# Products of a tile of zeros ahead of the first dense column and in the last norm

## The chip, the cores and the metric

The kernel runs on one core of a Trainium2 chip. The metric is the time of one execution on the device in microseconds (us); several executions are timed, and one is recorded by the profiler. The engines of the core are TensorE (PE, the matrix engine, whose weight loads are shown as PEld), VectorE (DVE), ScalarE (ACT), GpSimd (POOL) and SyncE (SP), which here issues nearly all DMAs. Each engine works through its own instructions in order.

## What is computed

Two layers of a decoder trunk on 512 tokens of width 1024, with 256 memory tokens; batch 1, all in f32. Cut to what matters:

```
for l in range(2):
    h = rmsnorm(x, norm_mix[l])
    p = h @ w_in[l]                        # columns: MLA | HGRN2 | S5 | RWKV-7 | 4 merge gates
    o_mla, o_hg, o_s5, o_rw = ...          # four token mixers on p, each 512 wide
    gates = sigmoid(gate_logits)           # 4 x 1024 columns of p
    y = (gates[0] * (o_mla @ w_branch_mla[l]) + gates[1] * (o_hg @ w_branch_hgrn[l])
         + gates[2] * (o_s5 @ w_branch_s5[l]) + gates[3] * (o_rw @ w_branch_rwkv[l]))
    x = x + y @ w_out[l]
    x = x + cross_attn(rmsnorm(x, norm_xq[l]), rmsnorm(mem, norm_xm[l]), ...)
    x = x + conv_ffn(rmsnorm(x, norm_ffn[l]), ...)
return rmsnorm(x, norm_final)
```

`mla` is causal latent attention with 4 heads: per head the scores of 4 query blocks of 128, a softmax, the transposed probabilities times the values.

## The kernel before

Activations lie transposed: a tile is 128 features by 512 tokens, 8 tiles for the width of 1024. All dense layers go through `dense`: the weights arrive in chunks of 8 blocks of 128 x 128 (`raw`, 512 KB, 3 buffers) in the one order in which they are used, ACT copies a chunk to a rounded half `whi` (L236), DVE makes the rest `wlo` (L237), and PE forms three products a block, L329 (`whi` times the high half of the activations), L330 (`whi` times the low half) and L331 (`wlo` times the high half). A column of 8 blocks is 24 products into one of two PSUM banks `mm`.

`run` begins with the load of the first chunk, the memory tokens (`mt`, halves `mh` and `ml`), and the 8 key columns of the memory for layer 0 (`early_keys`), whose products are 256 wide. `mixers` then walks the columns of the input projection in a fixed order; the mixers hang on it with priorities. After the mixers' columns come those of the gates (`gate`: copied by ACT at L556 to `g`, stored to `g_d`). `mla` runs when its columns are there. Its last steps for a head are: the softmax into the tiles `pr0` to `pr3`, transposes (L1574) into PSUM, copies `mpT` by ACT (L1575), four products with the values (L1578, bank `rwy`), a copy `mo` by ACT (L1580) and its store to `o_d[0]` in device memory.

`merge` follows. For each of the four mixers, in the order HGRN2, RWKV-7, MLA, S5, it loads the four tiles of the output (`oin`, 2 buffers), splits them into `oh` (ACT, L359) and `ol` (DVE, L360), loads a gate tile `gin` per column, applies a sigmoid on ACT (L574), and forms 8 columns of 4 blocks each. After it come cross attention, the feed-forward part, and in the end `final`: squares of `x`, four products with `ones` (L385), a short chain on DVE, four products that broadcast the result (L401), a scaling of 8 tiles and their stores.

A scheduler sets the order of all engines: it takes instructions by priority (by default their place in the code) as soon as it reckons them ready, so that work without inputs can stand far from where the code has it. Tiles live in pools. The constants, the activation halves, the ring of weights and the pools of the stages are stacked from the left of SBUF; some pools, that of `merge` (`mg`) among them, are stacked from the right. A pool whose memory was used by an earlier pool waits until that one is released, that is, until the last instructions that use its tiles are done. The pool of `mla` (`ml`) is on the left.

Of the kernel before, what the change touches and what calls it, by code (L numbers as in the profile page):

```python
# [9 lines left out]
F32 = mybir.dt.float32  # L10
# [12 lines left out]
P = 128  # L23
# [187 lines left out]
class Ring:  # L211


    def __init__(self, T, name, pool, raw_bufs, bufs):
        self.T, self.name, self.pool, self.rb, self.b = T, name, pool, raw_bufs, bufs
        self.n = CHUNK[name]
        self.order, self.dram, self.pos = ORDERS[name], T.A[name], 0
        self.raws = {}
# [32 lines left out]
class Trunk:  # L251
    def __init__(self, ctx, tc, A):
        self.tc, self.nc, self.A, self.ctx = tc, tc.nc, A, ctx
        nc = self.nc
        self.const = self.pool(ctx, "const")
        self.const.tile([P, 48], F32, name="pad0")
        self.hp = self.pool(ctx, "hp")
        self.sm = self.pool(ctx, "sm")
        self.sm.tile([P, 56], F32, name="pad1")
        self.pool(ctx, "pr", side="right").tile([P, 24], F32, name="pad2")  # L260
        self.ps = self.pool(ctx, "ps", space=PSUM)
        self.ring = Ring(self, "w", self.pool(ctx, "ring"), 3, 2)
        self.vec = self.const.tile([P, L, NVEC], F32, name="vec")
        nc.sync.dma_start(out=self.vec, in_=A["vec"])
        self.halves = self.const.tile([P, L, 24], F32, name="halves")
        o = VOFF["w0"]
        nc.vector.tensor_scalar(out=self.halves, in0=self.vec[:, :, o:o + 24], scalar1=0.5, scalar2=None, op0=ALU.mult)
        self.ident = self.const.tile([P, P], F32, name="ident")
        self.ones = self.const.tile([P, 1], F32, name="ones")
        nc.vector.memset(self.ones, 1.0)  # L270
        dp = self.pool(ctx, "dram", space=bass.MemoryType.DRAM)
        self.r_d = [dp.tile([3, 4, P, S], F32, name=f"r_d{l}") for l in range(L)]
        self.xk_d = [dp.tile([KD, P, MEM], F32, name=f"xk_d{l}") for l in range(L)]
        self.c_d = dp.tile([3, P, S], F32, name="c_d")
        self.su_d = dp.tile([4, P, 4, P], F32, name="su_d")
        self.sy_d = dp.tile([4, P, 4, P], F32, name="sy_d")
        self.x_d = dp.tile([KD, P, S], F32, name="x_d")
        self.o_d = [dp.tile([4, P, S], F32, name=f"o_d{m}") for m in range(4)]
        self.g_d = dp.tile([4, 8, P, S], F32, name="g_d")
# [420 lines left out]
    def ffn(self, l, pool):  # L700
# [3 lines left out]
        for half in range(2):  # L704
# [21 lines left out]
            for n in range(8):  # L726
                ps = self.dense([("down", l, half * FHALF + k, n) for k in range(FHALF)], lambda k: act[k])
                self.residual(ps, n)

    def final(self, out):  # L730
        nc = self.nc
        rs = self.rstd(self.x, D, S, self.xp)
        for j in range(KD):
            t = self.x[j]
            nc.vector.scalar_tensor_tensor(out=t, in0=t, scalar=self.v(0, "norm_final", j), in1=rs,
                                           op0=ALU.mult, op1=ALU.mult)
            self.dma(out[j], t)

    def run(self, out):
        A = self.A  # L740
        with ExitStack() as c:
            self.ring.load(0)
            kv = self.pool(c, "kv0")
            self.dma(self.ident, A["ident"])
            self.memory(0, kv, bufs=8)
            self.ring.load(1)
            self.xp = self.pool(c, "xp0")
            self.load_x(A["xT"], 2)
            self.early_keys(0, kv)
            with self.first(E0):  # L750
                self.norm_scaled(0, "norm_mix")
            self.constants(self.xp)
        for l in range(L):
            self.mixers(l)
            with ExitStack() as c:
                with ExitStack() as c2:
                    with ExitStack() as c3:
                        self.merge(l, self.pool(c3, "mg", side="right"))
                    self.xp = self.pool(c, "xp")
                    self.load_x(self.x_d if l else A["xT"])  # L760
                    kv = self.pool(c2, "kv")
                    self.memory(l, kv, True)
                    self.xk = [kv.tile([P, KD, MEM], F32R, name=f"xk{i}") for i in range(2)]
                    self.xv = [kv.tile([P, 2, D], F32R, name=f"xv{i}") for i in range(2)]
                    for n in range(8):
                        self.key_tile(l, kv, n)
                    for half in range(XV0[l]):
                        self.values(l, half)
                    for n in range(8):
                        ps = self.dense([("out", l, k, n) for k in range(KD)], self.h)  # L770
                        self.residual(ps, n)
                    with ExitStack() as c3:
                        self.xattn(l, kv, self.pool(c3, "xa", side="right"))
                with ExitStack() as c2:
                    self.ffn(l, self.pool(c2, "ff", side="right"))
                if l + 1 < L:
                    with ExitStack() as c2:
                        kv = self.pool(c2, "kv0")
                        self.memory(l + 1, kv)
                        self.early_keys(l + 1, kv)  # L780
                    for j in range(KD):
                        self.dma(self.x_d[j], self.x[j])
                    self.norm_scaled(l + 1, "norm_mix")
                else:
                    self.final(out)
# [891 lines left out]
```

## Time and profile before

| | us |
|---|---|
| median of 3 runs | 2731.95 (2727.4 to 2735.38) |
| the profiled execution | 2726.05 |
| its span, first to last instruction | 2724.2 |
| PE busy | 2662.7, 98% of the span |
| PE weight loads busy | 2168.2, 80% |
| DVE busy | 1816.5, 67% |
| ACT busy | 1114.3, 41% |

A row of the instructions in order of time reads: start in us, duration in us, engine, line, operation, output <- inputs, shape, count; in brackets the idle time of the engine ahead of it and what ended it. Matmuls overlap, so the distance between two starts tells the pace and not the duration.

### The profile page before, as it was taken

How to read it: one execution, taken by the hardware profiler on the slowest of the kernel's cores; microseconds unless marked ns; L12 is line 12 of the kernel's file. 1: busy time of each engine (PE TensorE's matmuls, PEld its weight loads, DVE VectorE, ACT ScalarE, POOL GpSimd, SP SyncE). 2: the span in 40 equal slices, each digit the busy share in tenths (PEclk: the TensorE clock that was granted, in tenths of full speed). 3: DMA queues.
4: the chain of work that ended last, by engine and by line, in shares of the span. 5: the costliest groups of instructions: out<-in, count | busy, mean ns of one | idle time of the engine just before them, and what ended most of it. 6: DMA issues, size and time to landing. Idle time of an engine off the chain costs nothing.

```text
span 2724.2 us, 37420 instructions
## 1 busy us (share of the span) xinstructions
PE 2662.7 (98%) x13920; PEld 2168.2 (80%) x13920; DVE 1816.5 (67%) x3826; ACT 1114.3 (41%) x1796; POOL 32.6 (1%) x117
## 2 busy tenths in 40 slices
PE   7999999999999999999999999999999999999997
PEld 6778877787788888888887787777877788888886
DVE  6588878876585566446475887888665945664563
ACT  5333353336654443223243334344465634332231
POOL 1000000000000000000000000000000000000000
PEclk9999999999999999999999999999999999999999
DMA  6332143344673233332443232333555632332332
GB/s 207 96 93 77 43 130 92 110 144 156 224 223 115 85 93 100 94 101 93 128 145 104 85 90 71 117 96 122 158 177 179 212 98 70 93 101 93 101 94 77
DMA packets 140134, 319.11 MB, mean 117 GB/s; under 512 B 20656, under 2 KB 42800, under 8 KB 139952
## 3 DMA queue, kind: packets, MB, share of 16 engines
q1 hardware_dynamic: 139952, 316.72, 37.3%
q8 instruction: 110, 1.80, 0.3%
q14 instruction: 72, 0.59, 0.1%
HBM read 266.06 MB, written 45.61 MB: 114 GB/s over the span
## 4 chain that ended last, share of the span: by engine, by line
PE 81%; DVE 10%; DMA 4%; ACT 2%; issue 2%; SPq 1%; DVEq 0%; POOL 0%; ACTq 0%; POOLq 0%
PE mm L330 20%; PE mm L329 20%; PE mm L331 20%; DVE wlo L237 2%; PE rw L1033 2%; PE hg L1396 1%; SPq L319 1%; DVE rdg L941 1%; PE rwy L658 1%; PE rw L658 1%; PE rw L1561 1%; DVE rdg L943 1%; ACT whi L236 1%; PE rw L1052 1%; PE mm L352 1%
## 5 line engine op out<-in xcount | busy, mean ns | idle before, releaser
L329 PE MATMUL mm<-hh,whi 128*128 128x512 f32 x2144 | 850.4, 397 | 3.4 <-ACT wa L471 2.5
L330 PE MATMUL mm<-hl,whi 128*128 128x512 f32 x2144 | 850.4, 397 | 0.0
L331 PE MATMUL mm<-hh,wlo 128*128 128x512 f32 x2144 | 849.0, 396 | 0.0
L236 ACT ACTIVATE whi<-raw 128x1024 fp32r<-128x1024 f32 (+1 forms) x402 | 417.8, 1040 | 740.0 <-PE mm L330 636.4
L237 DVE TENSOR_TENSOR wlo<-raw,whi 128x1024 fp32r<-128x1024 f32 (+1 forms) x402 | 481.3, 1198 | 294.0 <-ACT whi L236 287.8
L329 PEld LDWEIGHTS mm<-hh,whi 128*128 128x128 f32 x2144 | 404.3, 189 | 86.5 <-ACT wa L471 2.9
L330 PEld LDWEIGHTS mm<-hl,whi 128*128 128x128 f32 x2144 | 404.3, 189 | 83.1 <-issue 1.6
L331 PEld LDWEIGHTS mm<-hh,wlo 128*128 128x128 f32 x2144 | 404.4, 189 | 80.3 <-issue 1.5
L329 PE MATMUL mm<-ah,whi 128*128 128x512 f32 x352 | 136.9, 389 | 0.0
L330 PE MATMUL mm<-al,whi 128*128 128x512 f32 x352 | 136.9, 389 | 0.0
L331 PE MATMUL mm<-ah,wlo 128*128 128x512 f32 x352 | 136.9, 389 | 0.0
L587 DVE TENSOR_TENSOR x<-mm,x 128x512 f32<-128x512 f32 x64 | 44.2, 690 | 122.3 <-PE mm L331 122.3
L329 PE MATMUL mm<-oh,whi 128*128 128x512 f32 x256 | 100.9, 394 | 0.9 <-ACT mh L362 0.4
L331 PE MATMUL mm<-oh,wlo 128*128 128x512 f32 x256 | 100.1, 391 | 0.0
L330 PE MATMUL mm<-ol,whi 128*128 128x512 f32 x256 | 100.0, 391 | 0.0
L710 DVE TENSOR_TENSOR gt<-mm,rstd 128x512 f32<-128x512 f32 x44 | 30.5, 692 | 98.6 <-PE mm L331 94.7
L941 DVE TENSOR_TENSOR rdg<-rdg,rE 128x2 f32<-128x2 f32 (+30 forms) x248 | 83.9, 338 | 3.4
L717 ACT ACTIVATE cv<-cv 128x512 f32<-128x512 f32 x44 | 27.8, 632 | 129.7 <-DVE cv L715 129.7
L331 PEld LDWEIGHTS mm<-ah,wlo 128*128 128x128 f32 x352 | 66.1, 188 | 13.7
L329 PEld LDWEIGHTS mm<-ah,whi 128*128 128x128 f32 x352 | 66.1, 188 | 13.7
L330 PEld LDWEIGHTS mm<-al,whi 128*128 128x128 f32 x352 | 66.1, 188 | 13.7
L720 DVE TENSOR_TENSOR up<-mm,rstd 128x512 f32<-128x512 f32 x44 | 30.4, 691 | 63.9 <-PE mm L331 63.9
(516 smaller groups left out, 4008.9 us busy)
## 6 DMA issues: line engine op xcount, KB each, us to landing
raw<-w SPq DMA_DIRECT2D x384, 512.0 KB, 3.5
g_d<-g SPq DMA_DIRECT2D x64, 256.0 KB, 2.1
gin<-g_d SPq DMA_DIRECT2D x64, 256.0 KB, 3.7
oin<-o_d SPq DMA_DIRECT2D x32, 256.0 KB, 3.7
mt<-memT SPq DMA_DIRECT2D x32, 128.0 KB, 3.5
x<-xT SPq DMA_DIRECT2D x16, 256.0 KB, 5.4
raw<-wm SPq DMA_DIRECT2D x10, 256.0 KB, 2.8
xk_d<-xkt SPq DMA_DIRECT2D x16, 128.0 KB, 2.2
```

The source lines that it names most:

```text
L236: nc.scalar.activation(out=self.hi, in_=raw, func=AF.Copy)
L237: nc.vector.tensor_tensor(out=self.lo, in0=raw, in1=self.hi.bitcast(F32), op=ALU.subtract)
L329: nc.tensor.matmul(ps[:, :N], hi, xh, start=i == 0, stop=False)
L330: nc.tensor.matmul(ps[:, :N], hi, xl, start=False, stop=False)
L331: nc.tensor.matmul(ps[:, :N], lo, xh, start=False, stop=i == n - 1)
L587: self.nc.vector.tensor_tensor(out=self.x[n], in0=ps, in1=self.x[n], op=ALU.add)
L658: nc.tensor.matmul(out, x, y, start=first and n == 0, stop=last and n == 2)
L710: nc.vector.tensor_tensor(out=gt[:, 2:], in0=ps, in1=rs, op=ALU.mult)
L717: nc.scalar.activation(out=cv, in_=cv, func=AF.Silu)
L720: nc.vector.tensor_tensor(out=up, in0=ps, in1=rs, op=ALU.mult)
L941: V.tensor_tensor(out=tmp[:, :n, :t + 1], in0=M[:, :t + 1, :n].rearrange("p s c -> p c s"), in1=E[:, t, :t + 1].unsqueeze(1).to_broadcast( ...
L1033: PE.matmul(ps[:, cs], x[r0, cs], y[r0, cs], start=True, stop=True)
```

## The change

A tile of zeros, 128 x 256 in f32 (1024 bytes per partition), is added to the constants and set by DVE. `idle_products(n, w)` multiplies it by itself n times into the bank `hg`, which nothing reads afterwards. It is called with 5 products right behind the load of the first chunk, and with 3 at the beginning of `final`. Lines that follow are numbered higher in the changed kernel, by 2 to 10: L329, L359, L556, L574, L1574, L1578 and L1580 of before are L331, L361, L558, L576, L1584, L1588 and L1590; the new products are at L736.

```
+        self.zeros = self.const.tile([P, 256], F32, name="zeros")
+        nc.vector.memset(self.zeros, 0.0)
...
+    def idle_products(self, n, w):
+
+        ps = self.bank("hg")
+        for _ in range(n):
+            self.nc.tensor.matmul(ps[:, :w], self.zeros[:, :P], self.zeros[:, :w], start=True, stop=True)
+
     def final(self, out):
         nc = self.nc
+        self.idle_products(3, 256)
         rs = self.rstd(self.x, D, S, self.xp)
...
             self.ring.load(0)
+            self.idle_products(5, 256)
             kv = self.pool(c, "kv0")
```

The order of the built program differs from that of before in three regions: at the start of PE, where the five products stand first and behind a memset on DVE; and in both layers from the last part of `mla` to the middle of the cross attention's keys. What stands on PE at the end of `mla` in layer 1 (`rw<-ident,pr` are transposes, `mm<-hh` gate columns, `mm<-oh` merge columns), before:

```order
L331 MATMUL mm<-oh,wlo 128x512
L329 MATMUL mm<-oh,whi 128x512
L1574 MATMUL rw<-ident,pr 128x128 x3
L1578 MATMUL rwy<-mpT,vtok 128x512
L1578 MATMUL rwy<-mpT,vtok 128x384
L1578 MATMUL rwy<-mpT,vtok 128x256
L1578 MATMUL rwy<-mpT,vtok 128x128
L330 MATMUL mm<-ol,whi 128x512
```

And now, with the products of zeros written last in the code:

```order
L332 MATMUL mm<-hl,whi 128x512
L333 MATMUL mm<-hh,wlo 128x512
L736 MATMUL hg<-zeros 128x256
L1584 MATMUL rw<-ident,pr 128x128 x2
L1588 MATMUL rwy<-mpT,vtok 128x512
L736 MATMUL hg<-zeros 128x256
L1584 MATMUL rw<-ident,pr 128x128
L1588 MATMUL rwy<-mpT,vtok 128x384
L1588 MATMUL rwy<-mpT,vtok 128x256
L1588 MATMUL rwy<-mpT,vtok 128x128
L736 MATMUL hg<-zeros 128x256
L331 MATMUL mm<-oh,whi 128x512
```

Before, merge columns ran ahead of, between and behind the last products of `mla`; now gate columns stand ahead of them, the first merge column starts behind them, and the three products from `final` stand here. The last rows of PE, at the program's end, are as before.

The second place is the queue of SP in layer 1, where the merge's first loads `oin` stand (the names in brackets are semaphores: those of DMA queues, and of the engines). Before:

```order
L319 DMA raw<-w 128x1024 [waits DMAHW2_49,DVE_49]
L319 DMA oin<-o_d_94 128x512 [waits DMAHW3_49,DMAHW0_49,PE_49]
L319 DMA oin<-o_d_94 128x512 [waits DMAHW4_49]
L319 DMA gin<-g_d 128x512 [waits DMAHW5_49]
L319 DMA qp_17265<-qpl 64x512 [waits DMAHW6_49,DVE_49]
L319 DMA qp_17266<-qpl 64x512 [waits DMAHW7_49,DVE_49]
L319 DMA oin<-o_d_94 128x512 [waits DMAHW3_49,DVE_49]
```

And now:

```order
L321 DMA g_d<-g 128x512 [waits DMAHW3_49,Activation_49]
L321 DMA raw<-w 128x1024 [waits DMAHW4_49,DVE_49]
L321 DMA o_d_95<-mo 128x512 [waits DMAHW5_49,Activation_49]
L321 DMA oin<-o_d_96 128x512 [waits DMAHW5_49,DMAHW0_49,DMAHW6_49,PE_49,Pool_49]
L321 DMA oin<-o_d_96 128x512 [waits DMAHW7_49]
L321 DMA gin<-g_d 128x512 [waits DMAHW1_49]
L321 DMA gin<-g_d 128x512 [waits DMAHW2_49]
L321 DMA oin<-o_d_96 128x512 [waits DMAHW6_49,DMAHW3_49,DVE_49]
```

The first load of the merge stood ahead of the last parts of the queries (`qp`) of `mla`; now it stands right behind the store of its last head (`o_d<-mo`).

The third place is ACT in layer 0 behind the last head of `mla` (`whi` is a weight chunk's split, `g` a gate column's copy). Before:

```order
L1580 COPY mo<-rwy 128x512
L236 ACTIVATE whi<-raw 128x1024
L556 COPY g<-mm 128x512
L362 ACTIVATE mh<-mt,vec 128x256
L370 ACTIVATE sq<-mt 128x256
L236 ACTIVATE whi<-raw 128x1024
L556 COPY g<-mm 128x512
```

And now:

```order
L1590 COPY mo<-rwy 128x512
L236 ACTIVATE whi<-raw 128x1024
L558 COPY g<-mm 128x512
L361 ACTIVATE oh<-oin 128x512 x2
L576 ACT_TABLE_LOAD
L576 ACTIVATE gin<-gin 128x512 x3
L236 ACTIVATE whi<-raw 128x1024
L558 COPY g<-mm 128x512
```

The splits of the merge's first tiles and the sigmoids of its first gates, which had been done between the heads of `mla`, now stand between two weight splits.

## Rows read from the trace of the kernel before

**Rows 1.** The page: busy time of PE, and the chain that ended last.

```profile
PE 2662.7 (98%) x13920; PEld 2168.2 (80%) x13920; DVE 1816.5 (67%) x3826; ACT 1114.3 (41%) x1796; POOL 32.6 (1%) x117
...
PE 81%; DVE 10%; DMA 4%; ACT 2%; issue 2%; SPq 1%; DVEq 0%; POOL 0%; ACTq 0%; POOLq 0%
```

**Rows 2.** Stretches of 50 us from 1950 to 2200 us: busy time by engine, sum.

```profile
sum 250.00, PE 245.50 PEld 193.56 DVE 167.37 ACT 141.69 POOL 1.04; mean PE 49.10 PEld 38.71 DVE 33.47 ACT 28.34 POOL 0.21
```

**Rows 3.** PE in order of time, the first column and the second's start.

```profile
6.29 0.58 PE L329 MATMUL mm<-mh,whi 128*128 128x256 f32 x1 [6.29 <-ACT mh L362]
...
11.77 0.41 PE L331 MATMUL mm<-mh,wlo 128*128 128x256 f32 x1
...
12.26 0.28 PE L331 MATMUL mm<-mh,wlo 128*128 128x256 f32 x1
13.01 0.38 PE L329 MATMUL mm<-mh,whi 128*128 128x256 f32 x1 [0.47 <-ACT whi L236]
```

**Rows 4.** ACT in order of time, the split of the second chunk.

```profile
11.90 1.06 ACT L236 ACTIVATE whi<-raw 128x1024 fp32r<-128x1024 f32 x1 [1.32 <-DMA raw<-w]
```

**Rows 5.** PE in order of time, last dense product and L401.

```profile
2706.62 0.39 PE L331 MATMUL mm<-ah,wlo 128*128 128x512 f32 x1
...
2712.87 2.05 PE L401 MATMUL st<-ident,rsr 128*128 128x128 f32 x8 [2.52 <-DVE rsr L418]
```

**Rows 6.** PE in order of time, layer 1: end of `mla`, and a merge column.

```profile
2077.28 2.32 PE L1578 MATMUL rwy<-mpT,vtok 128*128 128x512 f32 x8
2079.35 0.48 PE L330 MATMUL mm<-ol,whi 128*128 128x512 f32 x1
...
2088.09 0.39 PE L329 MATMUL mm<-oh,whi 128*128 128x512 f32 x1
...
2090.81 0.39 PE L329 MATMUL mm<-oh,whi 128*128 128x512 f32 x1
```

**Rows 7.** ACT in order of time, the same place.

```profile
2079.64 0.59 ACT L1580 COPY mo<-rwy 128x512 f32<-128x512 f32 x1 [0.91 <-PE rwy L1578]
...
2097.89 1.33 ACT L359 ACTIVATE oh<-oin 128x512 fp32r<-128x512 f32 x2 [1.24 <-DMA oin<-o_d]
```

**Rows 8.** SP's issues in order of time, the same place.

```profile
2080.25 0.32 SPq L319 DMA_DIRECT2D o_d<-mo  x1
...
2082.40 0.80 SPq L319 DMA_DIRECT2D x<-x_d  x2
...
2094.75 0.92 SPq L319 DMA_DIRECT2D oin<-o_d  x2
```

**Rows 9.** DVE in order of time, the low half of a merge tile.

```profile
2098.55 0.69 DVE L360 TENSOR_TENSOR ol<-oin,oh 128x512 fp32r<-128x512 f32 x1 [0.90 <-ACT oh L359]
```

**Rows 10.** The tile `mo`: its stores.

```profile
DMA to landing us min/median/max: 2.0/2.2/3.2
```

**Rows 11.** The tile `oin`: its loads.

```profile
DMA to landing us min/median/max: 2.6/3.7/5.5
```

**Rows 12.** Stretches of 1 us: busy times, granted clock (third from the end).

```profile
1735.00:1736.00 1.00, 0.00 (x0) 0.00 (x0) 1.00 (x4) 0.77 (x2) 0.00 (x0) 0.89 0.96 389
...
1739.00:1740.00 1.00, 1.00 (x9) 0.86 (x7) 0.90 (x4) 0.46 (x1) 0.00 (x0) 0.90 0.92 340
```

**Rows 13.** ACT in order of time, layer 0: table, sigmoids, splits of chunks.

```profile
689.93 1.28 ACT L574 ACT_TABLE_LOAD   x1
...
695.65 1.70 ACT L574 ACTIVATE gin<-gin 128x512 f32<-128x512 f32 x3
...
717.46 1.06 ACT L236 ACTIVATE whi<-raw 128x1024 fp32r<-128x1024 f32 x1 [1.37 <-PE mm L330]
...
722.90 1.06 ACT L236 ACTIVATE whi<-raw 128x1024 fp32r<-128x1024 f32 x1 [1.94 <-PE mm L330]
```

**Rows 14.** PE in order of time, layer 0: tail of the last head.

```profile
707.66 0.44 PE L1574 MATMUL rw<-ident,pr 128*128 128x128 f32 x2
...
710.13 0.47 PE L330 MATMUL mm<-hl,whi 128*128 128x512 f32 x1
```

## The prediction

> **What bounds the kernel now.** I read the page first: TensorE (PE) is busy for 98% of the span and carries 81% of the chain that ended last [rows 1]. So time can be won or lost only where PE waits, and a wait is worth looking for to the microsecond. Then the stretches by 50 us: over 1950 to 2200 us, the end of layer 1's mixers and its merge, PE was busy for 245.5 of 250 us [rows 2]. All waits of that stage together are 4.5 us; nothing placed there can win more, while each new wait is paid in full. Last I read the three places that the change touches: the start, the last dense column, and, since the order of the built program differs there and nowhere else, the end of the latent attention (MLA) in both layers.
>
> **The five products at the start: 0.** The first dense product starts at 6.29 us and the column's last at 12.26 us [rows 3]. The products of zeros wait only for a memset on VectorE, which has nothing else to do before the first DMA lands. A 256-column f32 product costs 0.41 us at the full clock: four f32 products of 512, 384, 256 and 128 columns, 1280 in all, took from 2077.28 to 2079.35 us [rows 6], and 256/1280 of 2.07 us is 0.41 us. At half clock that is 0.83 us, and five end some 4.2 us after they begin, before 6.29 us. They can only make the first column end sooner, and the second column does not ask for that: its first product waited for `whi`, which ScalarE (ACT) started at 11.90 us when the weights' DMA landed, and PE went on at 13.01 us [rows 3, 4]. PE had been idle for 0.47 us there, and the early end only lengthens that idle time. I take 0, and keep 1 us of gain as the other bound.
>
> The Trainium skill, "TensorE: Matmul & The Clock Gate", section "Why this matters for your kernels", advises getting past the slow level with products ahead of the ones that count. Taken as a gain of time here, the 24 products of the first column would take 0.28 us each, as its last one does, and not 0.41 [rows 3]. That is at most 24 x 0.13, some 3 us, if the column bounded the second; by [rows 4] it does not, so I keep it only as a small chance.
>
> **The three products "behind the last dense column": 0, since they are not there.** The scheduler places by readiness, and these products need only the zeros. In the built program the last rows of PE are those of before (last column, then L385 and L401). The end chain therefore keeps its form: last dense product at 2706.62 us, the four broadcast products of L401 in 2.05 us [rows 5]. At the full clock these 4 x 128 f32 columns would take 4 x 0.21 = 0.83 us, so 1.2 us is all that this place could have given. The three stand in layer 1 instead, around the last products of the MLA (the first excerpt of the order in the change). Two stand between transposes, worth at most 0.8 us; ACT has to copy the transposes there in any case, which hides part. I take 0.4 us. The third stands behind the last L1578, in a wait.
>
> **The tile of zeros moves the memory: the large term.** 1024 bytes per partition more in the constants move all left-hand pools up. In the built programs the MLA's last tile (`pr3`) ended at byte 175200 before, and the merge's right-hand pool begins at 176000; now `pr3` ends at 176224. So the merge's tiles overlap the MLA's pool, and the first `oin` load waits until that pool is released: its counts are those of the last L1578 and of the store `o_d0<-mo` (read from the built program; the rows stand in the second excerpt). Before, it waited for work of the S5 mixer done long ago, and merge columns ran between the MLA's products. Now layer 1 has used up its gate columns when the MLA ends, and the next thing on PE is the merge's first column, in order, with nothing else to run.
>
> Step by step, from the rows of layer 1 at the same tail. PE is free at 2079.35 us [rows 6]. ACT's copy `mo` ends at 2079.64 + 0.59 = 2080.23 us [rows 7]; its store is issued at 2080.25 us. The release costs what it cost there already: `x<-x_d`, which waits for the same pool, was issued at 2082.40 us, 2.15 us later [rows 8]. A load `oin` issued at 2094.75 us let ACT begin its split at 2097.89 us, 3.14 us later [rows 7, 8]. So the split begins at 2085.54 us, `oh` is there 0.65 us later, and PE's first product starts near 2086.2 us. `ol` begins 0.66 us after `oh` and takes 0.69 us [rows 7, 9], to 2086.9 us. Only two `oin` buffers exist, so the third load waits for that `ol`: 2086.9 + 3.14 = 2090.0 us. The fourth goes 0.6 us later, and its split stands on ACT behind a sigmoid, so its `ol` is ready at about 2092.5 us and the first column ends at about 2093.0 us. Without a wait it takes from 2088.09 to 2090.81 us, 2.72 us [rows 6], and would end at 2079.35 + 2.72 = 2082.1 us. The stall is **10.9 us, taken as 11**. With the shortest landings (2.0 and twice 2.6 us) it is 9.7 us, with the longest (3.2 and twice 5.5 us) 16.7 us [rows 10, 11]; I stay near 3.14 us, since little else is loaded then. What is queued behind on SyncE (SP), the next weights among it, has three raw buffers ahead of it, so I count nothing for that.
>
> The Trainium skill, "DMA: Bandwidth & Descriptors", section "Anatomy of one DMA — SWDGE (gpsimd) path", gives about 2.0 us as the fixed cost of a DMA. By that alone the store and the two loads in a chain cost 6 us, against 8.4 us from the rows, and the stall would be 8.5 us (an estimate by that page). The rows hold the 256 KB as well, so I go by them.
>
> **The clock: 1.7 us.** From 1735 to 1736 us PE did nothing, and its granted clock fell: 0.89 in that slice, 0.50 in the three after it with PE busy again, 0.90 in the one from 1739 us [rows 12]. That is some 3.4 us at 1.2 GHz, so 1.7 us of work lost. A wait of 7 us, and a second of 3 us, should do the same. From 0 (the low time lies inside the stall) to 3.4 us (twice).
>
> **Layer 0: 1.2 us.** The same wait stands there, but four gate columns follow the MLA, 4 x 5.44 us [rows 13], and PE keeps running. ACT, though, works in order: behind the store it holds 2.15 + 3.14 us for the load, 1.33 us for two splits, 1.28 us for the table and 1.70 us for three sigmoids [rows 7, 8, 13], 9.6 us. In the new order a dense column ends just ahead of the tail of 2.47 us (707.66 to 710.13) [rows 14]. From that end, ACT is free after 2.47 + 0.9 + 9.6 = 13.0 us and has then to split (1.06) and to copy a gate (0.57): 14.6 us. PE asks for that after 2.47 + 2 x 5.44 = 13.35 us. 1.2 us late; from 0 to 4 us with slower loads.
>
> **Sum:** 11 + 1.7 + 0.4 + 1.2 = 14.3 us. Against the profiled execution, 2726.05 us (span 2724.2 us and 1.85 us around it), that is 2740.4 us. That execution lies 5.9 us under the median of the three runs, 2731.95 us; I add to the median: **2746 us**, slower by 0.52%. Some 0.3%, 8.2 us, is what a measurement of this kernel can tell from no change, that is 2723.8 to 2740.1 us.
>
> **Rivals.** *Not slower: the load is not late.* If the first `oin` is released well before PE gets to the merge, as before the change, the stall is gone: 2731.95 + 0.4 for the zeros and up to 1 us of gain at the start, about 2731 us. It decides at one point: the first load of layer 1 has to be issued some 8 us ahead of the last L1578. For it speaks only that the other loads of the merge are early now; against it that the row waits for the store, which comes behind that product. 0.10, of which 0.03 faster: the MLA's rows stand closer together, and a part of the 4.5 us of waits could go.
> *The short end.* Landings of 2.0 and 2.6 us, the clock's low time inside the stall, layer 0 covered: 9.7 - 1 = 8.7 us, less part of the old waits: 2739 us. 0.14.
> *The long end.* Loads like the slowest rows, two falls of the clock, ACT late in layer 0: 16.7 + 3.4 + 0.8 + 4 = 25 us, 2757 us. 0.10.
> *The warm start pays.* 14.3 - 3 us: 2743 us. By that rule; the trace speaks against it. 0.04.
> *The forecast:* 0.62.
>
> **How the numbers follow.** Slower by over 0.3%: forecast, long end and warm start, 0.62 + 0.10 + 0.04 = 0.76. Within 0.3%: the short end and most of the first rival, 0.14 + 0.07 - 0.01 = 0.20. Faster: 0.03, and 0.01 for a gain at both ends: 0.04. The range runs from 2735 us (the short end and the spread of the runs, 4 us) to 2757 us; the first rival is left out.
>
> **What would show it.** In the profile after: the five products end before the first dense one, and the second column still starts near 13 us on `whi`; nothing of zeros behind the last column and L401 still near 2 us; in layer 1 the first `oin` is issued some 2 us behind the last `o_d<-mo`, PE idles about 6 us and then about 3 us in the merge's first column, on `oh` and `ol`, and the clock is at half there; in layer 0 at most a short wait on `whi` or a gate's copy. I am wrong if PE runs on there, if the load goes out before the store, or if waits appear elsewhere.

## The result, and the profile after

The changed kernel takes **2752.36 us** (median of 6 runs, 2745.21 to 2758.95) against 2729.68 us for the kernel before in the same runs: ratio **1.0076, 95% interval 1.0057 to 1.0095**, slower by 0.76%. The prediction was 2746 us, slower by 0.52%, range 2735 to 2757 us. The profiled execution took 2756.97 us (span 2755.2 us). Over the runs of this study whose granted clock is on record, the changed kernel has a mean of 2751.0 us (23 runs) and the kernel before 2732.5 us (89 runs).

The page of the profile after, PE's busy time (in [rows 1] it was 2662.7 us).

```profile
PE 2688.2 (98%) x13936; PEld 2186.8 (79%) x13936; DVE 1817.9 (66%) x3827; ACT 1110.4 (40%) x1790; POOL 31.7 (1%) x117
```

PE is busy 25.5 us longer, and the products of zeros are only 6 us of that (4.35 us at the start, 0.6 us for each of the other three). So a good part of the loss is no waiting at all: PE does the same work more slowly in places.

*Start.* PE in order of time; the answer to [rows 3].

```profile
1.21 4.35 PE L736 MATMUL hg<-zeros 128*128 128x256 f32 x10 [1.21 <-DVE zeros L272]
6.33 0.39 PE L331 MATMUL mm<-mh,whi 128*128 128x256 f32 x1 [0.77 <-ACT mh L364]
...
7.81 0.28 PE L333 MATMUL mm<-mh,wlo 128*128 128x256 f32 x1
7.93 0.28 PE L331 MATMUL mm<-mh,whi 128*128 128x256 f32 x1
...
11.83 0.34 PE L333 MATMUL mm<-mh,wlo 128*128 128x256 f32 x1
12.80 0.39 PE L331 MATMUL mm<-mh,whi 128*128 128x256 f32 x1 [0.62 <-ACT whi L236]
```

(An f32 product stands as two records, hence x10 for five.) The five end at 5.56 us, before the first dense product. The dense ones then run 0.12 us apart at first, but 0.21 us apart from about 8.6 us on. The column ends 0.37 us earlier than before and the second column still waits for `whi`: it starts at 12.80 us, 0.21 us earlier.

*Layer 1, end of the MLA and start of the merge.* PE; the answer to [rows 6].

```profile
2088.64 1.02 PE L1588 MATMUL rwy<-mpT,vtok 128*128 128x512 f32 x2
2089.50 0.59 PE L736 MATMUL hg<-zeros 128*128 128x256 f32 x2
...
2090.22 1.46 PE L1588 MATMUL rwy<-mpT,vtok 128*128 128x384 f32 x6
2091.52 0.60 PE L736 MATMUL hg<-zeros 128*128 128x256 f32 x2
2098.60 0.79 PE L331 MATMUL mm<-oh,whi 128*128 128x512 f32 x1 [6.48 <-ACT oh L361]
...
2107.21 0.50 PE L331 MATMUL mm<-oh,whi 128*128 128x512 f32 x1
```

SP's issues, then ACT's work at the same place; the answer to [rows 7, 8].

```profile
2092.33 0.32 SPq L321 DMA_DIRECT2D o_d<-mo  x1
2095.21 0.79 SPq L321 DMA_DIRECT2D oin<-o_d  x2
...
2099.30 0.92 SPq L321 DMA_DIRECT2D oin<-o_d  x2
```

```profile
2091.72 0.59 ACT L1590 COPY mo<-rwy 128x512 f32<-128x512 f32 x1 [1.03 <-PE rwy L1588]
2097.91 1.22 ACT L361 ACTIVATE oh<-oin 128x512 fp32r<-128x512 f32 x2 [5.61 <-DMA oin<-o_d]
...
2102.80 0.63 ACT L361 ACTIVATE oh<-oin 128x512 fp32r<-128x512 f32 x1 [0.71 <-DMA oin<-o_d]
```

This is the chain of the prediction. The MLA's last product ends at 2091.68 us, the first `oin` goes out 2.88 us behind the store, its split begins 2.70 us later, and PE stands still for 6.48 us. The first two merge columns, 24 products or 5.5 us at 0.228 us each, are through at 2107.2 us: 15.5 us behind the MLA's last product, so the stall costs **10.0 us**. Before, there was no wait here [rows 6].

*End.* The answer to [rows 5]: the same form, nothing of zeros ahead of it, and L403 still at 2.05 us.

```profile
2743.76 2.05 PE L403 MATMUL st<-ident,rsr 128*128 128x128 f32 x8 [2.52 <-DVE rsr L420]
```

*The granted clock.* Stretches of the kernel after (columns: stretch, length, busy time of PE, PE weight loads, DVE, ACT, POOL with counts, granted clock, DMA share, GB/s), then one of the kernel before, as long and from about the same instruction on.

```profile
1763.00:1790.00 27.00, 27.00 (x153) 21.83 (x153) 11.95 (x25) 7.30 (x15) 0.00 (x0) 0.50 0.09 32
...
2098.00:2104.00 6.00, 5.40 (x11) 3.60 (x12) 1.83 (x3) 4.82 (x8) 0.00 (x0) 0.50 0.85 271
```

```profile
1757.00:1784.00 27.00, 27.00 (x227) 22.11 (x227) 19.81 (x43) 15.41 (x28) 0.00 (x0) 1.00 0.23 73
```

The half clock from 2098 us follows the new wait and was forecast. The one from 1763 us was not: for 27 us PE was busy without a break in layer 1's mixers (with products of 32x32 and 64x64 between the dense ones), at 0.50 (1.2 GHz), and got through 153 records where before it got through 227. That is some 12 us, at a place that the change does not touch.

*Where the time of this execution went.* The same products can be matched in the two traces and their starts compared. The kernel after falls behind by 11.9 us over the long fall of the clock, by 11.2 us over layer 1's merge, by 3.1 us over another fall at 1875 us and by 1.1 us over layer 0's merge. The other steps add up to some 3 us. So in this execution more was lost to the clock in stages that the change leaves alone than to the new wait.

### The profile page after: what moved, and what is told of

Read it like the earlier page. It is cut to its first block, busy times and chain, and to the rows that moved or that the text cites. A ratio compares the mean times of both kernels' runs of the same rounds, so it can differ in the third digit from the quotient of the medians.

```text
span 2755.2 us, 37440 instructions
## 1 busy us (share of the span) xinstructions
PE 2688.2 (98%) x13936; PEld 2186.8 (79%) x13936; DVE 1817.9 (66%) x3827; ACT 1110.4 (40%) x1790; POOL 31.7 (1%) x117
## 4 chain that ended last, share of the span: by engine, by line
PE 82%; DVE 10%; DMA 3%; ACT 2%; issue 2%; SPq 1%; DVEq 0%; POOL 0%; ACTq 0%; POOLq 0%
PE mm L332 20%; PE mm L331 20%; PE mm L333 20%; DVE wlo L237 2%; PE rw L1043 2%; PE hg L1406 1%; DVE rdg L951 1%; SPq L321 1%; PE rw L1571 1%; PE rwy L660 1%; PE rw L660 1%; DVE rdg L953 1%; ACT whi L236 1%; PE mm L354 1%; PE mm L353 1%
## 5 line engine op out<-in xcount | busy, mean ns | idle before, releaser
L331 PE MATMUL mm<-hh,whi 128*128 128x512 f32 x2144 | 854.8, 399 | 3.1 <-ACT wa L473 2.4
L331 PEld LDWEIGHTS mm<-hh,whi 128*128 128x128 f32 x2144 | 406.4, 190 | 87.1 <-ACT wa L473 2.9
L331 PE MATMUL mm<-ah,whi 128*128 128x512 f32 x352 | 136.9, 389 | 0.0
L331 PE MATMUL mm<-oh,whi 128*128 128x512 f32 x256 | 101.9, 399 | 7.4 <-ACT oh L361 6.5
L331 PEld LDWEIGHTS mm<-ah,whi 128*128 128x128 f32 x352 | 66.1, 188 | 13.8
```

What stands on the lines that cost most here:

```text
L331: nc.tensor.matmul(ps[:, :N], hi, xh, start=i == 0, stop=False)
```

## The experiments

Theory: the 1024 bytes push the MLA's pool into the merge's, so the first `oin` of layer 1 is late. First rival: the products of zeros cost the time themselves. Second rival: any shift of the addresses, or chance in the clock. "At 0.990" in the table is a kernel's time at a mean granted clock of 0.990, from a straight line through all 206 runs with one constant for each kernel (2.3 us for 0.001 of the clock, 2.0 us of scatter left).

| kernel | median us (runs) | ratio to before, 95% interval | at 0.990 |
|---|---|---|---|
| before | 2728.92 to 2733.12 (89) | 1 | 2734.1 |
| changed kernel, second set | 2750.84 (7) | 1.0060 (1.0038 to 1.0082) | 2741.8 (all 23) |
| changed kernel, third set | 2748.50 (10) | 1.0065 (1.0040 to 1.0091) | |
| unused tile of 1024 bytes | 2744.00 (10) | 1.0052 (1.0030 to 1.0074) | 2743.7 |
| unused tile of 768 bytes | 2732.89 (12) | 1.0001 (0.9981 to 1.0020) | 2734.4 |
| 15 products in the stall | 2747.44 (6) | 1.0046 (1.0031 to 1.0060) | 2746.6 |
| products, both pads out | 2770.95 (4) | 1.0137 (1.0118 to 1.0156) | 2772.0 |
| products, pads cut by 256 bytes | 2743.72 (12) | 1.0045 (1.0026 to 1.0064) | 2744.2 |
| the same, 12 products at the end | 2745.63 (12) | 1.0046 (1.0021 to 1.0072) | 2746.2 |
| ring of weights 32 bytes later | 2759.58 (2) | 1.0102 (1.0055 to 1.0149) | 2766.4 |
| `hh`, `hl` 64 bytes later | 2740.26 (12) | 1.0033 (1.0015 to 1.0052) | 2743.1 |
| products of 192 columns | 2732.99 (12) | 1.0014 (0.9994 to 1.0034) | 2733.5 |
| the same, 16 at the end | 2735.62 (12) | 1.0016 (0.9994 to 1.0038) | 2735.8 |

**1. The tile alone.**

```diff
+        self.const.tile([P, 256], F32, name="pad4")
```

> The kernel before with a tile of 1024 bytes per partition more in the constants, never written and never read; no product of zeros. Theory (memory: the merge's pool overlaps the latent attention's, so the first load of layer 1's merge waits for that pool's release): as slow as the changed kernel within 3 us, 12 to 25 us above before, with one wait of 6 to 7 us on oh in front of the merge's first column. Rival (the products cost it, by their place in the queue or by what they do to the clock): within 3 us of before, no such wait.

1.0052. PE at the merge (line numbers are one above those of before):

```profile
2095.30 1.02 PE L1579 MATMUL rwy<-mpT,vtok 128*128 128x512 f32 x2
2097.00 1.46 PE L1579 MATMUL rwy<-mpT,vtok 128*128 128x384 f32 x6
2105.14 0.80 PE L330 MATMUL mm<-oh,whi 128*128 128x512 f32 x1 [6.67 <-ACT oh L360]
```

The wait is there with no product in the kernel: the memory does it. The median lies 6.8 us under that of the changed kernel beside it, more than the 3 us expected; the clock differs, and at 0.990 the two agree within 2 us. The first two rows also price the product of zeros between the transposes: the two steps stand 1.70 us apart without it and 1.58 us with it in the kernel after. It costs nothing there; PE waits for the copies of the transposes instead.

**2. The same tile, 256 bytes smaller.** The MLA's last tile then ends at 175968, below 176000.

```diff
+        self.const.tile([P, 192], F32, name="pad4")
```

> The kernel before with an unused tile of 768 bytes where the other kernel had one of 1024; no product. The only difference between the two is whether the latent attention's last tile (now up to 175968) reaches over 176000, where the merge's pool begins. Theory (overlap): within 4 us of before, so 10 to 15 us faster than with 1024 bytes. Rival (any move of the addresses, or chance in the clock): as with 1024 bytes, 8 to 20 us above before.

1.0001, and the waits of PE from 2060 to 2140 us hold none on `oh`:

```profile
PE mm L330 <- ACT mh L363: 0.4, 1, 0.4
PE mm L330 <- DVE gin L580: 0.2, 1, 0.2
```

A shift that keeps the pools apart costs nothing; 256 bytes more cost 9 us at equal clock (2743.7 against 2734.4 us). The overlap is shown.

**3. The stall filled with products.**

```diff
-        self.idle_products(3, 256)
+        self.idle_products(18, 256)
```

> The changed kernel with 18 instead of 3 products of zeros in the second call; the scheduler sets 15 of them into the wait ahead of layer 1's first merge column, some 6.2 us of work for a wait of 6.5 us. What it tells apart is how much of the stall is the clock's: by the prediction's term 1.7 us (0 to 3.4), so the first two merge columns, which took 8.6 us from 2098.60 us in the changed kernel, should take 1.7 to 3 us less, at a granted clock of 1.00, and the kernel should stand 10 to 11 us above before in lag over this stretch instead of about 11 to 12. If the fall of the clock behind the wait costs nothing, the columns take as long as before. Rival (products in the queue make the time): slower than the changed kernel by about 6 us, as 15 products of 0.41 us are added.

PE at the merge:

```profile
2083.28 1.46 PE L1588 MATMUL rwy<-mpT,vtok 128*128 128x384 f32 x6
2084.59 6.64 PE L736 MATMUL hg<-zeros 128*128 128x256 f32 x30
2091.34 0.73 PE L331 MATMUL mm<-oh,whi 128*128 128x512 f32 x2
...
2096.46 0.73 PE L331 MATMUL mm<-oh,whi 128*128 128x512 f32 x2 [1.39 <-ACT oh L361]
...
2099.87 0.50 PE L331 MATMUL mm<-oh,whi 128*128 128x512 f32 x1
```

The granted clock stayed at 1.00 behind the stall:

```profile
2091.00:2097.00 6.00, 4.49 (x18) 2.77 (x16) 1.86 (x3) 4.67 (x8) 0.00 (x0) 1.00 0.94 290
```

Yet the first two merge columns, expected to take 1.7 to 3 us less than 8.6 us, take 8.5 us (2091.34 to 2099.87 us; 2098.60 to 2107.21 us in the kernel after): 0.1 us less. The third column starts 15.1 us behind the MLA's last product (2084.74 to 2099.87 us), as against 15.5 us; the other 0.3 us are the store's release, 2.57 us here and 2.88 us there. At full clock PE runs into the next wait, 1.39 us for the third `oin`; at half clock the same time went into slow products. In this stall the fall of the clock is covered by the loads. Its 15 products do not lengthen it either, against the rival.

**4. The products without the overlap, first try.** To win back the 224 bytes, the two unused pads were taken out.

```diff
-        self.const.tile([P, 48], F32, name="pad0")
-        self.sm.tile([P, 56], F32, name="pad1")
```

> The changed kernel without its two pads pad0 and pad1, 416 bytes less in front: all products of zeros are there, the pools stand apart as before (the latent attention's last tile ends at 175808, the merge's pool begins at 176000). Theory (memory): within 3 us of the kernel before, no wait over 3 us in layer 1's merge. Rival (products): 12 to 25 us above before, as the changed kernel. The scheduler now sets two of the three products behind the last dense column, so the two ends of the change are tried as they were meant: at the start the second column still waits for whi until about 12.8 us (gain 0.2 us); at the end the four broadcast products should take about 1 us where they took 2.05 us, if the two products keep the clock up over a wait of 2.3 us, and 2.05 us if not. Together 0 to 1.5 us of gain, less than the times can show.

1.0137, 38 us above before: both theories missed the time, though PE has no wait in layer 1's merge, as the first of them said, and the broadcast products at the end still take 2.05 us behind two products of zeros. The loss grows in the stretches of dense columns (some 3 us per 100 us from 1000 to 1300 us) and hardly in the mixers. Groups by shape, from 1000 to 1300 us: two of the kernel before, then one of this kernel (columns: count, busy us, mean ns of one, idle time):

```profile
L330 PE MATMUL mm<-hl,whi 128*128 128x512 f32 x351 | 136.6, 389 | 0.0
...
L329 PE MATMUL mm<-ah,whi 128*128 128x512 f32 x88 | 34.2, 389 | 0.0
```

```profile
L330 PE MATMUL mm<-al,whi 128*128 128x512 f32 x88 | 34.9, 396 | 0.0
```

Products overlap, so the mean of one is more than the pace. The six groups of the stretch (`hh` twice and `hl`, `ah` twice and `al`) hold 1315 products in 300 us before, 228 ns each, and 1278 here, 235 ns each, with no idle time in either. The pads had set addresses: without them the ring of weights (`raw`, `whi`, `wlo`), at multiples of 128 before, starts 32 bytes off. (`hh` and `hl` moved by 832 bytes as well, to 64 bytes off; experiment 6 comes back to that.)

**5. The ring moved, with all that lies behind it on the left; `hh`, `hl`, `ah` and `al` stayed.** Same instructions in the same order as before, no product.

```diff
-        self.sm.tile([P, 56], F32, name="pad1")
+        self.sm.tile([P, 64], F32, name="pad1")
```

> The kernel before with pad1 at 64 instead of 56 columns: everything behind it, the ring of weights among it, stands 32 bytes later; hh and hl, which lie ahead of it, stay; the instructions and their order are those of before. It asks whether the 38 us of the kernel without both pads, where the ring also stood 32 bytes off a multiple of 64, came from that. Theory (address): 512-column products every 234 ns instead of 227, some 30 to 40 us above before. Rival (the removed pads or the products did it in another way): 227 ns, within 4 us of before.

1.0102 (two runs, a wide interval), and again 1278 or so products (1279) in the same stretch, with the same means:

```profile
L330 PE MATMUL mm<-hl,whi 128*128 128x512 f32 x338 | 133.7, 395 | 0.0
...
L329 PE MATMUL mm<-ah,whi 128*128 128x512 f32 x88 | 34.8, 396 | 0.0
```

So the address costs the 7 ns, not the pads' absence and not the products; and since the streamed tiles of these groups stayed where they were, it is the address of the weights.

**6. The products without the overlap, second try.** The ring stands at multiples of 128 again.

```diff
-        self.const.tile([P, 48], F32, name="pad0")
...
-        self.sm.tile([P, 56], F32, name="pad1")
+        self.sm.tile([P, 40], F32, name="pad1")
```

> The changed kernel without pad0 and with pad1 cut from 56 to 40 columns: 256 bytes less in front, so that everything behind the constants stands 768 bytes later than before (a multiple of 64, as before) and the latent attention's last tile ends at 175968, below the merge's pool at 176000. All eight products are there, two of the last three behind the last dense column. Theory (the overlap costs it, not the products): within 4 us of before, layer 1's merge without a wait over 3 us, 512-column products every 227 ns. Rival 1 (the products cost it): 10 to 25 us above before. Rival 2 (the order with the pools apart costs the 38 us of the kernel without both pads, not the addresses): 25 to 40 us above before again.

1.0045: the first rival's forecast, and I took it for that at first. But the groups of the same stretch say otherwise:

```profile
L331 PE MATMUL mm<-hl,whi 128*128 128x512 f32 x347 | 135.6, 391 | 0.0
...
L331 PE MATMUL mm<-al,whi 128*128 128x512 f32 x88 | 34.2, 389 | 0.0
```

Products that stream `hh` or `hl` are slower, those that stream `al` are not. `hh` and `hl` lie between the two pads and moved by 832 bytes, so they start 64 bytes off a multiple of 128.

**7. Of the operands of the dense products only `hh` and `hl` moved** (with them the constants behind `pad0`), again with the instructions and the order of before.

```diff
-        self.const.tile([P, 48], F32, name="pad0")
+        self.const.tile([P, 64], F32, name="pad0")
-        self.sm.tile([P, 56], F32, name="pad1")
+        self.sm.tile([P, 40], F32, name="pad1")
```

> The kernel before with pad0 at 64 columns instead of 48 and pad1 at 40 instead of 56: hh and hl, which lie between the two, stand 64 bytes later, off a multiple of 128; the ring and all else stay, and so do the instructions and their order. Theory (address): products that stream hh or hl take 229 to 230 ns instead of 227, those that stream ah or oh 227; with some 6,000 such products 8 to 14 us above before. Rival (the products of zeros, or cut pads, made the 229 ns): 227 ns throughout, within 4 us of before.

1.0033, 9 us at equal clock, as in the second try, and the same pattern:

```profile
L330 PE MATMUL mm<-hl,whi 128*128 128x512 f32 x347 | 135.8, 391 | 0.0
L330 PE MATMUL mm<-al,whi 128*128 128x512 f32 x88 | 34.2, 389 | 0.0
```

**8. The products without the overlap, third try.** A tile of 768 bytes, all pads in place, so the addresses of experiment 2.

```diff
-        self.zeros = self.const.tile([P, 256], F32, name="zeros")
+        self.zeros = self.const.tile([P, 192], F32, name="zeros")
-            self.idle_products(5, 256)
+            self.idle_products(7, 192)
-        self.idle_products(3, 256)
+        self.idle_products(4, 192)
```

> The changed kernel with its tile of zeros cut to 192 columns (768 bytes), and 7 and 4 products of 192 columns in place of 5 and 3 of 256; all pads stay. The addresses are those of the kernel with the unused tile of 768 bytes, 1.0001 of before; pools apart, hh and the ring at multiples of 128 as before. Two of the four last products stand behind the last dense column. Theory (the 11 us of the kernel with pads cut and all products came from hh standing 64 bytes off a multiple of 128, its dense products at 229 to 230 ns, and not from the products): within 4 us of before, hh products at 227 ns. Rival (the products cost about 11 us by themselves): 8 to 15 us above before, with hh products at 227 ns and the loss in waits or in the clock.

1.0014, no difference clear of noise; 2733.5 us at 0.990 against 2734.1 us. At equal clock the products cost nothing. As the runs stand, a cost of a few us is not excluded: these 12 runs and the 12 of the kernel with 16 products have a mean 4.4 us above that of the kernel before beside them (standard error 2.0 us), at a mean clock of 0.9894 against 0.9909. With the pools apart the scheduler sets two of the last four where the change wanted them. The end of this kernel:

```profile
2705.52 0.40 PE L333 MATMUL mm<-ah,wlo 128*128 128x512 f32 x1
2705.76 0.81 PE L736 MATMUL hg<-zeros 128*128 128x192 f32 x4
2708.24 1.02 PE L387 MATMUL st<-ones,sq 128*128 128x1 f32 x8 [1.67 <-DVE sq L375]
2711.79 2.05 PE L403 MATMUL st<-ident,rsr 128*128 128x128 f32 x8 [2.53 <-DVE rsr L420]
```

They bring nothing: behind them PE still waits twice, and L403 takes its 2.05 us. From the last dense product to L403's end it is 8.32 us, before 8.30 us [rows 5].

**9. More products at the end**, first with the pads cut (12 products), then with the tile of 192 columns:

```diff
-        self.idle_products(4, 192)
+        self.idle_products(16, 192)
```

> As the kernel with the pools apart and all products, but 12 products in the second call instead of 3. The scheduler sets 5 of them behind the last dense column, ahead of L386, 5 more into the wait of 2.5 us between L386 and the broadcast products of L402, and one behind these. If products in that second wait keep the clock up, the four broadcast products take about 0.8 to 1.0 us where they took 2.05 us, and the end comes about 1.1 us sooner; if five products (2.05 us at the full clock) come late or the clock falls all the same, they take 2.05 us. In the time this is less than can be measured: within 4 us of before.

> As the one before it, with 16 products of 192 columns in the second call: 7 behind the last dense column, 7 in the wait between L387 and the broadcast products of L403. The broadcast products should take 1.0 to 1.2 us (2.05 without), and the end, from the last dense product to theirs, 7.4 us (8.30 in the kernel before): 0.9 us of gain, which the time cannot show: within 4 us of before. Rival (the products cost): 8 to 15 us above.

The time shows nothing, as expected (1.0016; the 1.0046 of the 12 products is that of experiment 6). With 12 products L402 takes 1.13 us. The end of the kernel with 16:

```profile
2708.82 0.40 PE L333 MATMUL mm<-ah,wlo 128*128 128x512 f32 x1
2709.05 2.44 PE L736 MATMUL hg<-zeros 128*128 128x192 f32 x14
2711.54 1.02 PE L387 MATMUL st<-ones,sq 128*128 128x1 f32 x8
2712.43 2.52 PE L736 MATMUL hg<-zeros 128*128 128x192 f32 x14
2715.10 1.13 PE L403 MATMUL st<-ident,rsr 128*128 128x128 f32 x8
```

Both waits are full, L403 takes 1.13 us, and the end 7.41 us instead of 8.30 us: 0.9 us are there to be had, by products in the wait just ahead of the ones that count. That is the most that was got out of this place, and too little to make a version that measurably beats the kernel before.

**10. The changed kernel again, twice.**

> The changed kernel once more, as the measure for the runs beside it. Both theories: some 15 to 25 us above the kernel before (1.0057 to 1.0095). If the stretch of half clock at 1763 to 1790 us in layer 1's mixers is a matter of chance, the profile lacks it or has it elsewhere, and the times spread by more than 8 us with the mean granted clock; if the change causes it, it stands at the same place again.

> The changed kernel a third time, for one open point: at the same mean granted clock the changed kernel stands some 9 us above before, the rest of its 15 to 25 us goes with a lower mean clock (0.9863 in 6 and 0.9864 in 7 runs, 0.990 to 0.991 in the 74 runs of before). If the lower clock belongs to the kernel, it comes again at 0.985 to 0.988 and the ratio at 1.006 to 1.008; if it was chance, the mean clock lies at 0.989 or above (the stall itself, 6.8 us at half clock, accounts for 0.0012) and the ratio at 1.003 to 1.005.

1.0060 and 1.0065. The mean clock came low both times, 0.9864 and 0.9855 after 0.9863 in the first set, against 0.9907 over the 89 runs of before. The third set was to tell chance from the kernel, and the low clock came again, so it belongs to this kernel. The long fall at 1763 us is no fixed part of it. Stretches of the second set's profile, of the third's, and of the kernel with the unused 768 bytes, each from about the same place in layer 1's mixers:

```profile
1767.00:1793.00 26.00, 26.00 (x208) 21.26 (x207) 18.36 (x40) 12.62 (x22) 0.00 (x0) 0.92 0.18 54
```

```profile
1767.00:1793.00 26.00, 26.00 (x150) 20.93 (x150) 11.95 (x25) 6.26 (x13) 0.00 (x0) 0.50 0.09 31
```

```profile
1755.00:1782.00 27.00, 27.00 (x153) 21.73 (x152) 11.95 (x25) 7.26 (x15) 0.00 (x0) 0.50 0.09 30
```

It stands in one of them in full, in one hardly, and it also stands in a kernel that is as fast as before.

## Why the prediction was right, and by how much it was off

*Start, 0:* right; 0.2 us, inside the 1 us kept, and by 50 us into the kernel nothing of it is left (0.1 us behind). The rival of the warm start fell (its 24 x 0.13 us also took durations for the pace; by the starts, 0.21 and 0.12 us apart, it is 24 x 0.09, some 2 us): the first dense products did run at full pace, 0.12 us apart, but only until 8.6 us, and the column's end was not what the second column waited for. The Trainium skill, "TensorE: Matmul & The Clock Gate", section "Why this matters for your kernels", advises warming up with matmuls before what is measured; this trace agrees that they bring the pace, and shows that it was gone before the column was through and was not needed.

*Products not behind the last column, 0:* right, and so is the bound of 1.2 us for that place: 0.9 us when it is really filled (experiment 9). *Two products between transposes, 0.4 us:* 0 (experiment 1).

*The memory, 11 us:* the mechanism is shown by experiments 1, 2 and 8, and its size was good: 10.0 us. The parts erred both ways: release 2.88 us for 2.15, load to split 2.70 us for 3.14 (3.50 us for the third load, 2099.30 to 2102.80 us). Release and both loads make 9.1 us, nearer to the 8.4 us from the rows than to the 6 us set beside them, whose 2.0 us are given for DMAs that GpSimd issues; SP issued these. One step was wrong in its form. I let the first column run "in order, with nothing else to run" into a second wait of 3 us; in the built program the products of the second column on the first two tiles stand in between, and at half clock they filled that wait. So the clock was no addition here: 0.1 us (experiment 3) where I had put 1.7 us on top.

*Layer 0, 1.2 us:* about right in size (1.1 us by the starts of the same products). Stretches of 100 us from 700 us on, of the kernel before and of the kernel after:

```profile
700.00:800.00 100.00, 99.61 (x444) 80.84 (x443) 70.72 (x126) 54.51 (x93) 0.00 (x0) 1.00 0.71 230
```

```profile
700.00:800.00 100.00, 98.24 (x436) 78.65 (x435) 67.47 (x124) 57.44 (x98) 0.00 (x0) 1.00 0.79 254
```

PE was busy 1.4 us less. But the wait was not where I put it, on `whi` or a gate's copy. It is the norm behind the first `oh` columns that waits for its squares:

```profile
PE st L387 <- DVE sq L375: 1.5, 1, 1.5
```

*The sum.* What the mechanisms give is 10.0 + 1.4 - 0.2 = 11.2 us (by the starts of the same products, 11.2 + 1.1 = 12.3 us). At a clock of 0.990 the kernels with the overlap stand 7.7 us (changed), 9.6 us (tile alone) and 12.5 us (18 products) above before. The first two have the stall's 6.8 us at half clock, which lower the mean by half of 6.8 in 2750 us, 0.0012, and cost no time; the straight line credits 2.8 us for it. With these given back it is 10.5, 12.4 and 12.5 us, so the 11 to 12 us are borne out. The forecast of 14.3 us lay above that, and the measured 18.5 us (mean of 23 runs against mean of 89) above the forecast. **The term that was mis-sized is the clock**: I priced it as two short falls in the merge, 1.7 us with 3.4 us as the end. The mean granted clock went down by 0.0047 over the whole kernel; without the stall's part it is 0.0035, at 2.3 us for 0.001 some 8 us. The falls behind it sit in other stages, behind waits of PE that the kernel before has too: in layer 1's mixers PE waits 1.52 us for `rdg` at 1759.7 us and the clock then falls for 27 us; before, it waited 1.58 us at the same instruction and kept the clock.

That the range held the time is thus partly luck: the merge was a little cheaper than forecast and the clock much dearer. One thing was missing altogether: I looked at the addresses for the overlap alone and read the pads as unused space. The 1024 bytes happen to keep every operand where it was against 128; a shift like those of experiments 4 and 6 would have cost 9 to 38 us, and no rival held that.

*Open:* how the overlap and the products lower the clock in stages that they do not touch. The mean clock of the kernels with neither is 0.9907 (115 runs), with the products and the pools apart 0.9896 (52 runs; the standard error of the difference is 0.0005), with the tile alone 0.9875 (10 runs), with both, the changed kernel, 0.9860 (23 runs); with 18 products, which leave no fall in the stall, 0.9898 (6 runs). So most of what is missing comes with the overlap and some with the products: 0.0032 and 0.0011 make 0.0043 of the 0.0047. The 0.0015 between the changed kernel and the tile alone are about their standard error (0.0014) and need no cause of their own. The same PE waits lead to a fall in some executions and not in others, and no run here steers that.

## What to carry over

A tile added to a constant pool moves every pool behind it: before costing what the tile is for, lay the addresses of both builds side by side and look for pools that now overlap and for operands that lose their alignment. A filler product goes where the scheduler first finds the engine free, so its place has to be read from the built program; it helps only in the wait directly ahead of the work that is to run fast. And where some 0.3% is at stake, compare runs at equal mean clock to find a cause, since the clock moves a run of this kernel by more than that; but the cost of a change is its time as it stands, the clock that it brings along included.

## What the runs showed of the hardware

A dense product of 512 columns takes 228 ns here (mean over 1000 to 1300 us) when the ring of weights stands at multiples of 128 bytes and 235 ns when it stands 32 bytes off (experiments 4 and 5). With the ring in place and the streamed `hh` and `hl` 64 bytes off, the products that read them take some 230 ns and the others 228 (300 us hold 1305 products instead of 1315; experiments 6 and 7). It matters what the moved tile is used for: in the kernel of experiment 5 the products that stream `whi` against `mh`, both 32 bytes later, keep 0.227 us from start to start (six in 1.36 us from 825.98 us on), right behind dense ones at 0.233 us. A ring 64 bytes off wasn't tried. The Trainium skill, "SBUF — State Buffer", section "Operand start alignment", asks only for a multiple of the element's size and says that its rule is about legality, not speed; these runs measure the speed: 0.3% to 1.0% of the kernel with not one instruction changed. Which unit is behind it, the runs don't show.

At the start the products of zeros take 0.87 us each (five in 4.35 us), half the pace, while the profile grants a clock of 1.00. The first stretch below is theirs; in the second, from 8.6 us on, the clock is granted at 0.50 and the dense products stand 0.21 us apart. In the kernel before they stand as far apart there with 1.00 granted. So at the start the granted clock does not tell the pace: the trace's first record of it stands at 5.1 us in the kernel after, towards the end of the products of zeros, and at 12.1 us in the kernel before, where the pace rises from 0.21 to 0.12 us; ahead of that record the profile prints 1.00.

```profile
1.20:5.60 4.40, 4.35 (x10) 3.19 (x10) 1.33 (x9) 1.80 (x3) 0.06 (x1) 1.00 0.87 271
...
8.60:11.90 3.30, 3.30 (x17) 3.30 (x16) 1.70 (x5) 1.15 (x4) 0.00 (x0) 0.50 0.92 306
```
